# Retention's query and key projections as wide groups behind the visited ones, with the gate projections visited in their place

## The chip, the cores and the metric

The kernel runs on one core of one Trainium2 chip. The metric is the device time of one execution in microseconds, lower is better; the time before is the median of 3 runs. Times of single instructions, of waits and of stretches come from one execution taken by the hardware profiler.

The engines are called as the profile calls them: PE is the matrix engine (PEld its weight loads), DVE the vector engine, ACT the scalar engine, POOL the general-purpose engine, SP the queue that issues nearly all transfers. SBUF is the on-chip memory with 128 partitions; PSUM is the memory in eight banks into which PE writes, one bank holding 512 float32 columns.

## What is computed

One decoder layer with two token mixers and a gated convolutional feed-forward part, for 256 tokens of width 2048, in float32. The part that matters here is the projection `h @ w_in` and what takes its columns:

```python
h = modulate(rms_norm(x, g_norm1[l]), shift1, scale1)
p = h @ w_in[l]
rq, rk, rv, rg, hq, hf, hi, hg, ga, gb = jnp.split(p, split_at, axis=-1)

q_r = rope(rq.astype(f32).reshape(B, S, RET_H, RET_DK), positions)
k_r = rope(rk.astype(f32).reshape(B, S, RET_H, RET_DK), positions)
o_r = head_layer_norm(retention_chunkwise(q_r, k_r, v_r)).reshape(B, S, RET_H * RET_DV)
y_a = (o_r.astype(x.dtype) * jax.nn.silu(rg)) @ w_ret_o[l]
...
o_h = head_rms_norm(hgrn2_chunkwise(q_h, f_g, hi)).reshape(B, S, HG_H * HG_DV)
y_b = (o_h.astype(x.dtype) * jax.nn.silu(hg)) @ w_hg_o[l]

merged = jax.nn.sigmoid(ga) * y_a + jax.nn.sigmoid(gb) * y_b
x = x + gate1[:, None, :] * (merged @ w_out[l])
```

Each of rq, rk, rv, rg, hq, hf, hi, hg has 1024 columns, ga and gb 2048 each. `shift1` and `scale1` come from `silu(c) @ w_ada`, which is another 2048 x 12288 matrix. After this part come the second norm, the up projection with a causal convolution of three taps, and the down projection.

## The kernel before

**Number format.** Weights are read as float32. Each piece of weights is split into an upper part `wh` (ACT copies it to the format that PE multiplies fast, line 167) and a rest `wl` (DVE subtracts, line 172). Activations are split likewise, and lie side by side in one tile: `act[:, :T]` are the upper parts of all 256 tokens, `act[:, T:]` the rests. A product is upper times upper, rest of the activation times upper weight, and upper activation times rest of the weight; rest times rest is left out.

**Groups, pieces, buffers.** A group is 512 columns of a weight matrix, and has 16 k tiles of 128 rows. `pieces` (line 176) fetches two k tiles at a time: a DMA into one of 12 `raw` buffers, then `wh` and `wl` into one of 4 buffers each. A buffer is free again when the last matmul that reads it is done.

**Three forms of matmul.** `mm_rows` (190) keeps 128 tokens of an activation as the stationary operand and streams 512 columns of weights: for each k tile and each half of the tokens, upper and rest of the activation against `wh`, and the upper one against `wl`, so 6 matmuls of 512. The result has tokens in partitions. `mm_cols` (203) keeps 128 columns of weights and streams 256 tokens, 12 matmuls of 256 for each k tile; the result has columns in partitions, as rope and the scores want it. The up projection (`up_group`, 1071) has a third form: the weights are stationary, upper and rest of the activation are streamed together in one matmul of 512, and one matmul of 256 with `wl` follows; upper and rest land in two halves of a bank and are added when the bank is read.

**PSUM.** `pg` (89) gives a pair of banks, two pairs in all; `po` (95) gives one bank, four in all.

**The visited stage** (lines 837 to 869). `scale1` and `shift1` are made row by row on DVE from the transposed `w_ada`, two k tiles of the activation hT at a time, and projections start before hT is complete. The twelve groups of the tuple ATT are visited in turn; each visit multiplies the k tiles that are there and not yet done (1 to 5 of them), and `take` (790) adds the bank pair to the group's sum `accs[g]` in SBUF: ACT copies on the first visit, DVE adds on the later ones. When hT is complete, the groups are finished in the order of their number. The four groups in ROWS use `mm_rows`, the other eight `mm_cols`. As soon as the three groups of an HGRN2 half, or of a retention half, are finished, its generator is put into a background queue.

**Background.** `pump` is called after each pair of k tiles and takes steps of the generators in the queues by an estimate of their time, so that their instructions lie between those of the projections. Queue 0 is first in, first out: trigonometry, `hgrn` for two halves, `retention` for two halves, then the gating. Queue 1 has the products with `w_ada`. An instruction of the background stands in its engine's order like any other.

**Behind the visits** (874 to 898). The groups of `wb` (the gate projections hg and rg) run one after the other in `mm_rows` form, 16 k tiles each into one bank pair, and ACT writes Silu of the pair into a tile `gt` (883). Eight groups of `wab` for the branch gates follow in the same manner with Sigmoid (897). `hgrn` waits with its last part until its gate is there (670); `gating` multiplies retention's output by its gates.

**Tiles.** Sums, gates, rope's scratch, HGRN2's scratch and the like are blocks of 4 KiB per partition, of which there are 27 (`blk`, 73). A block is given back when the program drops its last name for it.

Of the kernel before, what the change touches and what calls it, by code (L numbers as in the profile page):

```python
# [16 lines left out]
AF = mybir.ActivationFunctionType  # L17
ALU = mybir.AluOpType

P = 128  # L20
D = 2048
T = 256
NT = T // P
KT = D // P
# [5 lines left out]
G = 512  # L30
# [8 lines left out]

C_RQ, C_RK, C_RV, C_RG, C_HQ, C_HF, C_HI, C_HG = (i * W1 for i in range(8))  # L40
C_GA, C_GB = 8 * W1, 8 * W1 + D
ATT = (C_HF, C_HF + G, C_HQ, C_HQ + G, C_HI, C_HI + G, C_RQ, C_RQ + G, C_RK, C_RK + G, C_RV, C_RV + G)
ROWS = (C_HI, C_HI + G, C_RV, C_RV + G)
GW = 2 * G
LEVELS = (64, 32, 16, 8, 4, 2, 1)
TWO_PI = 2.0 * math.pi
# [9 lines left out]
class Kernel:  # L56
# [146 lines left out]
    def mm_cols(self, ps, items, first, last):  # L203

        nc = self.nc
        cs = [slice(j * P, (j + 1) * P) for j in range(4)]
        outs = [ps[j // 2][:, j % 2 * T : (j % 2 + 1) * T] for j in range(4)]
        for i, (act, wh, _) in enumerate(items):
            for j in range(4):

                opens = first and i == 0 and j % 2 == 0
                nc.tensor.matmul(outs[j], lhsT=wh[:, cs[j]], rhs=act[:, :T], start=opens, stop=False, skip_group_check=True)  # L212
                nc.tensor.matmul(outs[j], lhsT=wh[:, cs[j]], rhs=act[:, T:], start=False, stop=False, skip_group_check=True)  # L213
        for i, (act, _, wl) in enumerate(items):
            for j in range(4):
                nc.tensor.matmul(outs[j], lhsT=wl[:, cs[j]], rhs=act[:, :T], start=False, stop=last and i == len(items) - 1, skip_group_check=True)  # L216

    def products(self, mm, ps, src, act, k0, kts, hold=0, first=True, last=True, gain=None):

# [306 lines left out]
    def hgrn(self, hb, hf, hq, v, gates):  # L526

        nc = self.nc

        f = self.blk([P, 4, T], name="f")  # L530
        k = self.blk([P, 4, T], name="k")
        b = self.blk([P, 4, T], name="b")
        nc.scalar.activation(f, hf, AF.Sigmoid)
        yield 3.0
        for h in range(4):
            g = slice(4 * hb + h, 4 * hb + h + 1)
# [16 lines left out]
        f = None  # L553
        q = self.blk([P, 4, T], name="q")
        nc.scalar.activation(q, hq, AF.Silu)
        yield 2.0
        at = self.blk([P, 4, T], name="at")
        nc.gpsimd.memset(at, 0.0)
# [9 lines left out]
        ps = self.po()  # L568
# [5 lines left out]
        ps = self.po()  # L574
# [4 lines left out]
        for c in range(2):  # L579
            dst = at[:, :, c * P : (c + 1) * P].rearrange("p h (z x) -> p h z x", x=32)  # L580
            msk = self.ident.bitcast(I32).rearrange("p (z x) -> p z x", x=32)[:, None].to_broadcast([P, 4, 4, 32])
            src = ps[:, 4 * c * 32 : 4 * (c + 1) * 32].rearrange("p (h x) -> p h x", h=4)[:, :, None, :].to_broadcast([P, 4, 4, 32])
# [3 lines left out]
        kt = self.blk([P, 4, T], name="kt")  # L586
        nc.gpsimd.memset(kt, 0.0)
        for lev, n in enumerate(LEVELS[:-2]):
# [15 lines left out]
            ps = self.po()  # L604
            for h in range(4):
                for c in range(2):
                    j = 2 * h + c
# [11 lines left out]
            if n >= 32:  # L619
                for z in range(0, P, 2 * n):  # L620
                    for c in range(2):
                        dst = at[z : z + n, :, c * P + z + n : c * P + z + 2 * n]
                        src = ps[z + c * n : z + (c + 1) * n, : 4 * n]
# [28 lines left out]
        ps = self.po()  # L652
        for z in range(2):
            for j in range(4 * z, 4 * z + 4):
                h, c = j // 2, j % 2
                for x in range(0, P, 32):
# [3 lines left out]
                        lhsT=kt[:, h, c * P + x : c * P + x + 32],  # L660
                        rhs=eq[:, j, :].rearrange("p (l x) -> p l x", l=2)[:, :, x // 2 : x // 2 + 16],
                        start=True,
                        stop=True,
# [3 lines left out]
            self.masked(at, len(LEVELS) - 2 + i, n, ps[:, : 8 * 32].rearrange("p (j l x) -> p j l x", j=8, l=2)[:, :, i, :])  # L667
            yield 0.9
        yield 2.8
        while len(gates) <= hb:  # L670
            yield None
        o = self.blk([P, NT, G], name="oh")
        for t in range(NT):
            ps = self.po()
# [85 lines left out]
    def run(self):  # L760
        nc, a = self.nc, self.a
# [23 lines left out]

        accs = [self.blk([P, NT, G] if c0 in ROWS else [P, 4, T], name="p") for c0 in ATT]
        done = [0] * len(ATT)
        mms = [self.mm_rows if c0 in ROWS else self.mm_cols for c0 in ATT]

# [14 lines left out]
        ps = [self.po2(), self.po2(), self.pg(), self.pg()][:FIRST]  # L804
        for k in range(2):
# [12 lines left out]
            for g in range(FIRST):  # L818
                if g >= ahead:
                    rests.append(self.rest(uppers[g] if g < len(uppers) else self.upper(a["wa"][g][:, k : k + 1, :], 1, G)))  # L820
                wh, wl = rests[g]
# [14 lines left out]

        work = 2 * FIRST
        g = FIRST
        att, gates = [], []
        small = False  # L840
        while min(done) < KT:
            if work > SMALL and not small:
                small = True
                self.small_loads(nc.sync, ("freq", "lbT", "lmask"))
                self.start(self.trig())
                self.start(self.lower_bound())
            have = min(KT, 2 + int((work - LAG) / ADA_EVERY))
            m = have - done[g]
            if m > 0:
                self.finish(*ada[:have])  # L850
                if g < RESIDENT:
                    self.products(mms[g], ps[g], a["wa"][g], act, done[g], m, first=False, last=have == KT)
                    if have == KT:
                        take(g, ps[g], True)
                else:
                    take(g, self.products(mms[g], self.pg(), a["wa"][g], act, done[g], m), done[g] == 0)
                done[g] = have
                work += m
                for hb in range(2):
                    for kind, first in ((self.hgrn, 0), (self.retention, 6)):  # L860
                        gs = [first + hb, first + 2 + hb, first + 4 + hb]
                        if g in gs and min(done[i] for i in gs) == KT:
                            self.pace(0, 14.0, 24)
                            att.append(self.start(kind(hb, *(accs[i] for i in gs), gates)))
            else:
                work += 0.5
            g = (g + 1) % len(ATT)
            if have == KT and done[0] < KT:
                g = min(i for i in range(len(ATT)) if done[i] < KT)
        self.xT = None  # L870
        del accs
        self.small_loads(nc.sync, ("gn2", "convw"))

# [2 lines left out]
        self.pace(0, 143.0, 88)  # L876
        self.pace(1, 68.0, 96)
        sgb, sga = [], []
        for j in range(4):
            ps = self.rows(a["wb"][j], act)  # L880
            gt = self.blk([P, NT, G], name="gt")
            for at, z in ps:
                nc.scalar.activation(gt[:, at, :], z, AF.Silu)
            gates.append(gt)

        og = [[], []]

# [6 lines left out]
        for j in range(8):  # L894
            gt = self.blk([P, NT, G], name="gt")
# [40 lines left out]
        for j in range(4):  # L936
            last = j == 3
            x1.append(self.load_rows(j))
            if not last:
                g = self.row(self.gate["gate1"], j, "g1")  # L940
            if j == 2:
                g3 = self.row(self.gate["gate1"], 3, "g1")
            elif last:
                g = g3
            ps = self.products(self.mm_rows, self.po2() if last else self.pg(), a["wout"][j], actm, 0, KT, hold=4 * last, gain=g if last else None)
            if last:
                g = None
# [49 lines left out]
        steps = []  # L997
# [173 lines left out]
def _pack(w):  # L1171

    k, n = w.shape
    return np.ascontiguousarray(w.reshape(k // P, P, n).transpose(1, 0, 2))


def _groups(w, starts):
    return np.stack([_pack(w[:, s : s + G]) for s in starts])
# [23 lines left out]
def _arrays(x, c, positions, w_ada, b_ada, g_norm1, w_in, w_ret_o, w_hg_o, w_out, hg_lb, g_norm2, w_up, conv_w, conv_b, w_down, g_final):  # L1202
    cols = lambda v: np.ascontiguousarray(v.reshape(-1, P).T)
    wada, win, wup = w_ada[0], w_in[0], w_up[0]
    out = {
        "xT": _pack(np.ascontiguousarray(x[0].T)),
        "c": c.reshape(1, D),
        "pos": positions.reshape(1, T),
        "gn1": cols(g_norm1[0]),
        "gn2": cols(g_norm2[0]),  # L1210
        "lbT": np.ascontiguousarray(hg_lb.reshape(2, HH, P).transpose(2, 0, 1)),
        "convw": np.ascontiguousarray(np.concatenate([conv_w[0], conv_b], axis=0).reshape(4, 2 * FT, P).transpose(2, 0, 1)),
        "gf": g_final.reshape(1, D),
        "xR": np.ascontiguousarray(x[0].reshape(NT, P, D).transpose(1, 0, 2)),
        "wb": _groups(win, [C_HG, C_HG + G, C_RG, C_RG + G]),
        "wab": _groups(win, [z + j * G for z in (C_GB, C_GA) for j in range(4)]),
        "whg": _groups(w_hg_o[0], [j * G for j in range(4)]),
        "wret": _groups(w_ret_o[0], [j * G for j in range(4)]),
        "wout": _groups(w_out[0], [j * G for j in range(4)]),
        "wdown": _groups(w_down[0], [j * G for j in range(4)]),  # L1220
        "wup": np.stack([_pack(np.concatenate([wup[:, 2 * i * P : 2 * (i + 1) * P], wup[:, FF + 2 * i * P : FF + 2 * (i + 1) * P]], axis=1)) for i in range(FT // 2)]),
    }
    out["wa"] = _groups(win, ATT)
    adaT = np.concatenate([wada.T, b_ada[0][:, None]], axis=1).reshape(6, KT, P, D + 1)
    out["ada1"] = np.ascontiguousarray(adaT[[1, 0]].transpose(1, 0, 2, 3))
    out["ada2"] = np.ascontiguousarray(adaT[[4, 3]].transpose(1, 0, 2, 3))
    out["gate1"] = adaT[2]
    out["gate2"] = adaT[5]
    out.update(_tables())
    return out  # L1230
# [22 lines left out]
```

## Time and profile before

| what | value |
|---|---|
| median of 3 runs | 1513.63 us (1513.56 to 1513.67) |
| profiled execution | 1513.78 us |
| its span, first to last instruction | 1512.0 us |
| mean granted PE clock | 0.998 |
| instructions | 23190 |
| busy: PE, DVE, ACT | 1496.0, 1206.4, 846.6 us |
| read from memory | 382.11 MB, 254 GB/s over the span |

How to read the rows that follow. A row of the waits names the engine and line that waited, then what it waited for, the total in us, the number of times and the longest. A row of the timeline has the start in us from the span's beginning, the duration, the engine, the line, the operation, what it writes and reads, and in brackets how long the engine was idle before it and what ended that. A row of the groups has line, engine, operation, tiles, shapes and count, then busy time in us and the mean duration in ns, then the idle time of the engine before these instructions. A row of the stretches has, for each engine, the busy time in us and in brackets the number of instructions that ran in it, then the granted clock, the DMAs' share and GB/s. Matmuls are pipelined: a recorded matmul of 256 columns lasts longer than the distance to the next one's start, so the cost of a matmul in a run of them is that distance.

### The profile page before, as it was taken

The numbers are of one execution on the slowest core, as the hardware profiler recorded it, in microseconds if no ns is written. First come the engines' busy times: TensorE is split into PE (matmuls) and PEld (weight loads), VectorE is DVE, ScalarE is ACT, GpSimd is POOL, SyncE is SP. The second block draws the span as 40 slices with busy tenths as digits, with TensorE's granted clock in tenths as the row PEclk, the third lists the DMA queues.
The fourth block names the chain that finished last, engine by engine and source line by source line (L and its number), as shares of the span: only waits on it lengthen the run. The fifth ranks groups of instructions, "written<-read, shape, count | busy, mean of one in ns | idle before, by whom it ended". The sixth has DMA issues, their size and how long they took to land.

```text
span 1512.0 us, 23190 instructions
## 1 busy us (share of the span) xinstructions
PE 1496.0 (99%) x8722; PEld 1288.2 (85%) x8722; DVE 1206.4 (80%) x1639; ACT 846.6 (56%) x1207; POOL 4.0 (0%) x8
## 2 busy tenths in 40 slices
PE   8999999999999999999999999999999999999997
PEld 6999999888888888888888888888888888888886
DVE  7899996997999877898977778778777769455794
ACT  6655454777875644455466555555655558344342
POOL 0000000000000000000000000000000000000000
PEclk9999999999999999999999999999999999999999
DMA  9999997777888889989847777777777766667651
GB/s 374 390 332 340 315 326 230 258 265 251 286 269 289 281 299 326 320 286 362 305 126 244 233 232 230 231 229 236 227 244 230 218 192 204 194 206 214 185 168 56
DMA packets 110996, 385.75 MB, mean 255 GB/s; under 512 B 12802, under 2 KB 13346, under 8 KB 110884
## 3 DMA queue, kind: packets, MB, share of 16 engines
q1 hardware_dynamic: 110016, 383.14, 76.8%
q8 instruction: 68, 1.11, 0.3%
q10 hardware_dynamic: 868, 1.13, 0.2%
q14 instruction: 44, 0.36, 0.1%
HBM read 382.11 MB, written 2.11 MB: 254 GB/s over the span
## 4 chain that ended last, share of the span: by engine, by line
PE 95%; DVE 3%; DMA 1%; ACT 1%; issue 0%; SPq 0%; DVEq 0%; ACTq 0%
PE pg L196 13%; PE pg L197 13%; PE pg L201 13%; PE po L1086 11%; PE pg L1086 10%; PE po L1088 5%; PE pg L1088 5%; PE po L201 3%; PE po L197 3%; PE po L196 3%; PE pg L212 3%; PE pg L213 3%; PE pg L216 3%; PE po L212 1%; PE po L213 1%; PE po L216 1%
## 5 line engine op out<-in xcount | busy, mean ns | idle before, releaser
L167 ACT ACTIVATE wh<-raw 128x1024 fp32r<-128x1024 f32 (+1 forms) x536 | 550.1, 1033 | 514.8 <-PE pg L197 181.1
L172 DVE TENSOR_TENSOR wl<-raw,wh 128x1024 fp32r<-128x1024 f32 (+1 forms) x536 | 634.0, 1189 | 236.0 <-ACT wh L167 232.7
L426 DVE SCALAR_TENSOR_TENSOR raw<-raw,sc 128x1024 f32<-128x1024 f32 x192 | 233.6, 1219 | 0.0
L1086 PE MATMUL po<-h2T,wh 128*128 128x512 f32 x704 | 221.1, 395 | 0.0
L1086 PE MATMUL pg<-h2T,wh 128*128 128x512 f32 x688 | 216.4, 396 | 0.0
L196 PE MATMUL pg<-wh,hT 128*128 128x512 f32 x512 | 202.8, 396 | 0.2 <-ACT p L794 0.2
L197 PE MATMUL pg<-wh,hT 128*128 128x512 f32 x512 | 200.0, 391 | 0.0
L1088 PEld LDWEIGHTS po<-h2T,wl 128*128 128x128 f32 x704 | 132.3, 188 | 31.2
L1088 PEld LDWEIGHTS pg<-h2T,wl 128*128 128x128 f32 x688 | 129.1, 188 | 31.1 <-DVE wl L172 0.5
L1088 PE MATMUL po<-h2T,wl 128*128 128x256 f32 x704 | 138.3, 278 | 0.0
L201 PE MATMUL pg<-wl,hT 128*128 128x512 f32 x512 | 137.4, 390 | 0.0
L1088 PE MATMUL pg<-h2T,wl 128*128 128x256 f32 x688 | 135.3, 278 | 0.1
L201 PEld LDWEIGHTS pg<-wl,hT 128*128 128x128 f32 x512 | 96.0, 188 | 20.4 <-DVE wl L172 0.2
L196 PEld LDWEIGHTS pg<-wh,hT 128*128 128x128 f32 x512 | 96.2, 188 | 19.9 <-ACT p L794 0.4
L197 PEld LDWEIGHTS pg<-wh,hT 128*128 128x128 f32 x512 | 96.2, 188 | 19.1
L1086 PEld LDWEIGHTS po<-h2T,wh 128*128 128x128 f32 x704 | 107.2, 189 | 0.0
L1086 PEld LDWEIGHTS pg<-h2T,wh 128*128 128x128 f32 x688 | 104.7, 189 | 0.0
L212 PE MATMUL pg<-hT,wh 128*128 128x256 f32 x384 | 95.2, 284 | 0.6 <-DVE p L796 0.6
L213 PE MATMUL pg<-hT,wh 128*128 128x256 f32 x384 | 95.1, 284 | 0.0
L212 PEld LDWEIGHTS pg<-hT,wh 128*128 128x128 f32 x384 | 74.1, 193 | 1.1 <-issue 0.8
L213 PEld LDWEIGHTS pg<-hT,wh 128*128 128x128 f32 x384 | 74.0, 193 | 0.3
L197 PE MATMUL pg<-wh,gs 128*128 128x512 f32 x176 | 68.6, 390 | 0.0
(250 smaller groups left out, 2062.7 us busy)
## 6 DMA issues: line engine op xcount, KB each, us to landing
raw<-in_wup SPq DMA_DIRECT2D x176, 512.0 KB, 4.4
raw<-in_wdown SPq DMA_DIRECT2D x88, 512.0 KB, 4.3
raw<-in_wa SPq DMA_DIRECT2D x80, 512.0 KB, 5.7
raw<-in_ada SPq DMA_DIRECT2D x64, 512.5 KB, 5.8
raw<-in_ada SPq DMA_DIRECT2D x64, 512.0 KB, 5.6
raw<-in_wab SPq DMA_DIRECT2D x64, 512.0 KB, 4.9
raw<-in_gate SPq DMA_DIRECT2D x32, 512.5 KB, 4.2
raw<-in_wb SPq DMA_DIRECT2D x32, 512.0 KB, 4.7
```

The lines of the kernel that those rows point to most:

```text
L167: self.pin(self.nc.scalar.activation(wh, raw, AF.Copy))
L172: self.last = self.nc.vector.tensor_tensor(wl, raw, wh.bitcast(F32), ALU.subtract)
L196: nc.tensor.matmul(ps[t], lhsT=act[:, hi], rhs=wh, start=first and i == 0, stop=False)
L197: nc.tensor.matmul(ps[t], lhsT=act[:, lo], rhs=wh, start=False, stop=False)
L201: nc.tensor.matmul(ps[t], lhsT=act[:, hi], rhs=wl, start=False, stop=last and i == len(items) - 1)
L212: nc.tensor.matmul(outs[j], lhsT=wh[:, cs[j]], rhs=act[:, :T], start=opens, stop=False, skip_group_check=True)
L213: nc.tensor.matmul(outs[j], lhsT=wh[:, cs[j]], rhs=act[:, T:], start=False, stop=False, skip_group_check=True)
L216: nc.tensor.matmul(outs[j], lhsT=wl[:, cs[j]], rhs=act[:, :T], start=False, stop=last and i == len(items) - 1, skip_group_check=True)
L426: dot = self.pin(nc.vector.scalar_tensor_tensor(raw[:, 0, :], raw[:, 0, :], 1.0, self.sc[:, u * GW : u * GW + w], ALU.mult, ALU.mult, accu ...
L1086: self.pin(nc.tensor.matmul(ps[j + z], lhsT=wh[:, cs[z]], rhs=act, start=kt == 0, stop=False, skip_group_check=bool(begun)))
L1088: nc.tensor.matmul(ps[j + z][:, :T], lhsT=wl[:, cs[z]], rhs=act[:, :T], start=False, stop=kt == KT - 1, skip_group_check=bool(begun))
```

## The change

ATT loses the four query and key groups of retention (`C_RQ`, `C_RK`) and gets the four gate groups in their places; the gates are visited in rows form, and when one is complete, ACT applies Silu to its sum in place. `gates` becomes a dictionary by number, and `hgrn` waits for its number in it. The names of `hf` and `hq` are dropped as soon as HGRN2 has read them.

Behind the visits, `wide_group` makes the four query and key groups, one after the other, in the wide form: both bank pairs belong to one group, four k tiles are taken at a time, and for each pair of banks the eight matmuls of 512 with `wh` come first and the eight of 256 with `wl` after them. Then each pair is evicted by an ACT copy of the half with the rests and a DVE addition of the upper half. After the second group the first half of retention is started, after the fourth the second. The host packs the four groups as `wk` in place of `wb`.

```diff
-ATT = (C_HF, C_HF + G, C_HQ, C_HQ + G, C_HI, C_HI + G, C_RQ, C_RQ + G, C_RK, C_RK + G, C_RV, C_RV + G)
-ROWS = (C_HI, C_HI + G, C_RV, C_RV + G)
+GATES = (C_HG, C_HG + G, C_RG, C_RG + G)
+ATT = (C_HF, C_HF + G, C_HQ, C_HQ + G, C_HI, C_HI + G, *GATES, C_RV, C_RV + G)
+ROWS = (C_HI, C_HI + G, *GATES, C_RV, C_RV + G)
+KEYS = (C_RQ, C_RK, C_RQ + G, C_RK + G)
...
+    def mm_wide(self, ps, items, first, last, pair):
+        nc = self.nc
+        for i, (act, wh, _) in enumerate(items):
+            for z in (pair, pair + 1):
+                nc.tensor.matmul(ps[z], lhsT=wh[:, z * P : (z + 1) * P], rhs=act, start=first and i == 0, stop=False)
+        for i, (act, _, wl) in enumerate(items):
+            for z in (pair, pair + 1):
+                nc.tensor.matmul(ps[z][:, :T], lhsT=wl[:, z * P : (z + 1) * P], rhs=act[:, :T], start=False, stop=last and i == len(items) - 1)
+
+    def wide_group(self, src, act):
+        nc = self.nc
+        pgs = [self.pg(), self.pg()]
+        ps = pgs[0][:2] + pgs[1][:2]
+        steps = list(range(0, KT, 4))
+        pieces = self.pieces(src, KT)
+        for k in steps:
+            items = [(act(kt), wh, wl) for _ in range(2) for kt, wh, wl in next(pieces)]
+            for pair in (0, 2):
+                self.mm_wide(ps, items, k == 0, k == steps[-1], pair)
+                self.pump()
+        out = self.blk([P, 4, T], name="p")
+        for pair in (0, 2):
+            dst = out[:, pair : pair + 2, :]
+            z = pgs[pair // 2][2]
+            nc.scalar.activation(dst, z[:, :, T:], AF.Copy)
+            nc.vector.tensor_tensor(dst, dst, z[:, :, :T], ALU.add)
+        return out
...
         nc.scalar.activation(f, hf, AF.Sigmoid)
+        hf = None
...
         nc.scalar.activation(q, hq, AF.Silu)
+        hq = None
...
-        while len(gates) <= hb:
+        while hb not in gates:
             yield None
...
+                if have == KT and ATT[g] in GATES:
+                    nc.scalar.activation(accs[g], accs[g], AF.Silu)
+                    gates[GATES.index(ATT[g])] = accs[g]
                 for hb in range(2):
-                    for kind, first in ((self.hgrn, 0), (self.retention, 6)):
-                        gs = [first + hb, first + 2 + hb, first + 4 + hb]
-                        if g in gs and min(done[i] for i in gs) == KT:
-                            self.pace(0, 14.0, 24)
-                            att.append(self.start(kind(hb, *(accs[i] for i in gs), gates)))
+                    gs = [hb, 2 + hb, 4 + hb]
+                    if g in gs and min(done[i] for i in gs) == KT:
+                        self.pace(0, 14.0, 24)
+                        begin(self.hgrn, hb, *(accs[i] for i in gs))
+                        for i in gs:
+                            accs[i] = None
...
-        for j in range(4):
-            ps = self.rows(a["wb"][j], act)
-            gt = self.blk([P, NT, G], name="gt")
-            for at, z in ps:
-                nc.scalar.activation(gt[:, at, :], z, AF.Silu)
-            gates.append(gt)
+        for hb in range(2):
+            begin(self.retention, hb, *[self.wide_group(a["wk"][2 * hb + i], act) for i in range(2)], v.pop(0))
```

More of the change, by code (lines that the diff above doesn't have):

```diff
@@ L838, in run, with begin @@
         g = FIRST
-        att, gates = [], []
+        att, gates = [], {}
+        def begin(kind, hb, *ins):
+            att.append(self.start(kind(hb, *ins, gates)))
         small = False
@@ L870, in run @@
         self.xT = None
+        v = accs[10:]
         del accs
@@ L1214, in _arrays @@
         "xR": np.ascontiguousarray(x[0].reshape(NT, P, D).transpose(1, 0, 2)),
-        "wb": _groups(win, [C_HG, C_HG + G, C_RG, C_RG + G]),
+        "wk": _groups(win, KEYS),
         "wab": _groups(win, [z + j * G for z in (C_GB, C_GA) for j in range(4)]),
```

## The prediction

> **What bounds the kernel now.** I read the page first: the span, the busy time of each engine and the chain that ended last.
>
> ```profile
> span 1512.0 us, 23190 instructions
> ...
> PE 1496.0 (99%) x8722; PEld 1288.2 (85%) x8722; DVE 1206.4 (80%) x1639; ACT 846.6 (56%) x1207; POOL 4.0 (0%) x8
> ...
> PE 95%; DVE 3%; DMA 1%; ACT 1%; issue 0%; SPq 0%; DVEq 0%; ACTq 0%
> ```
>
> PE is busy for 99% of the span and is 95% of the chain. A busy PE can still be waiting inside its pipeline, so the next view is that of the waits, for PE alone over the whole run (total, times, longest).
>
> ```profile
> engine line waited for: us in total, times, longest us
> PE po L264 <- DMA crow<-in_c: 2.3, 1, 2.3
> PE po L212 <- ACT hT L350: 1.9, 2, 1.2
> PE po L317 <- DVE rq L313: 1.6, 1, 1.6
> PE pg L1065 <- DVE h2T L398: 0.7, 1, 0.7
> PE po L618 <- DVE kt L602: 0.6, 1, 0.6
> PE pg L212 <- DVE p L796: 0.6, 1, 0.6
> PE pg L196 <- ACT p L794: 0.2, 1, 0.2
> PE po L213 <- DVE hT L355: 0.2, 1, 0.2
> ```
>
> These add up to 8.1 us, 5.8 of them in the three rows at the top, which belong to the start. So there is almost no idle time to win: the time is the number of matmuls times the distance between their starts. A change gains if it issues fewer or cheaper matmuls, and loses if DVE, ACT or the DMAs can no longer keep the next operands ready. How near those are to that point is read by stage. The visited stage runs to about 295 us, the four gate groups from there to about 390.
>
> ```profile
> core 0: us, PE busy (x) PEld busy (x) DVE busy (x) ACT busy (x) POOL busy (x), PEclk, DMA share, GB/s
> 20.00:100.00 80.00, 78.92 (x542) 73.68 (x542) 69.16 (x97) 49.79 (x75) 0.00 (x0) 1.00 1.00 371
> 100.00:180.00 80.00, 80.00 (x577) 75.96 (x576) 77.24 (x107) 43.33 (x63) 1.91 (x2) 1.00 0.97 339
> 180.00:260.00 80.00, 80.00 (x588) 76.47 (x588) 66.12 (x80) 37.33 (x54) 0.00 (x0) 1.00 0.85 281
> 260.00:293.00 33.00, 32.39 (x203) 29.14 (x202) 26.79 (x31) 26.21 (x30) 0.00 (x0) 1.00 0.71 231
> 293.00:335.00 42.00, 42.00 (x353) 34.24 (x352) 41.15 (x55) 29.35 (x42) 0.00 (x0) 1.00 0.83 276
> 335.00:377.00 42.00, 42.00 (x379) 34.65 (x378) 34.35 (x50) 33.21 (x54) 1.92 (x2) 1.00 0.76 255
> ```
>
> The granted clock is 1.00 in every stretch. DVE is 97% busy (77.24 of 80) from 100 to 180 us and 98% (41.15 of 42) from 293 to 335: those are the two narrow places. The DMAs moved 371 GB/s in the first stretch and 339 in the second, so there the bytes aren't at their limit.
>
> **The matmuls.** What one k tile (128 rows of weights, 512 columns) costs PE in each of the three forms is read from the timeline of PE, as the distance from one pair of k tiles to the next.
>
> ```profile
> 227.61 0.28 PE L212 MATMUL pg<-hT,wh 128*128 128x256 f32 x1
> ...
> 230.49 0.28 PE L212 MATMUL pg<-hT,wh 128*128 128x256 f32 x1
> ```
>
> Columns form (mm_cols, queries and keys now): 24 matmuls of 256 between these starts, 2.88 us, so 1.440 us per k tile and 0.120 each.
>
> ```profile
> 302.04 0.39 PE L196 MATMUL pg<-wh,hT 128*128 128x512 f32 x1
> ...
> 304.75 0.39 PE L196 MATMUL pg<-wh,hT 128*128 128x512 f32 x1
> ```
>
> Rows form (mm_rows, the gates before and after): 12 matmuls of 512, 2.71 us, so 1.355 per k tile and 0.226 each.
>
> ```profile
> 839.66 0.62 PE L1086 MATMUL pg<-h2T,wh 128*128 128x512 f32 x2
> 840.13 0.40 PE L1088 MATMUL pg<-h2T,wl 128*128 128x256 f32 x2
> ...
> 842.45 0.62 PE L1086 MATMUL po<-h2T,wh 128*128 128x512 f32 x2
> ```
>
> The up projection has the wide form that the change gives to queries and keys: 8 matmuls of 512 and 8 of 256 in 2.79 us, so 1.395 per k tile. All three forms stream 3072 columns per k tile; what differs is the number of matmuls, 12, 6 and 8. Two rows give both prices: if 0.120 is 256c+o and 0.226 is 512c+o, c is 0.414 ns and o 14 ns. Every matmul saved is worth about 14 ns, not its load of weights, which hides.
>
> The change turns 4 groups of 16 k tiles, 64 in all, from 12 matmuls into 4 of 512 and 4 of 256. In runs of eight like ones, as the new order issues them, the two single prices give 4x0.226+4x0.120=1.384; the up rows, the same mix in shorter runs, say 1.395. The saving is 64x(1.440-1.384)=3.6 us or 64x(1.440-1.395)=2.9. I take the middle, **3.2 us**. The gates cost 1.355 in either place. By stage: the visited one loses 64x(1.440-1.355)=5.4 us of PE, and what follows gains 64x(1.39-1.355)=2.2.
>
> The Trainium skill, page "TensorE: Matmul & The Clock Gate", section "Back-to-back issue gap", gives an isolated gap of N/2.4 ns plus 2.5 at full clock. By that an estimate for the k tile is 1.310 us in columns form and 1.300 in the wide form, and the saving would be 0.6 us in place of 3.2. The rows here have 14 ns where the page has 2.5, so the sum goes by the rows.
>
> **What else moves.** The visited stage still makes the same 53 visits with the same k tiles in each (counted by stepping through the loop of lines 841 to 869), one eviction per visit, and the same background work tied to k tiles and not to time. Its transfers are as many and as large; the SP queue only has the gate groups' loads where the query and key groups' were. A round of the twelve groups at one k tile takes 8x1.440+4x1.355=16.94 us now and 16.60 after, 2.0% less, in which DVE, ACT and DMA must do as much. DVE at 97% would be at 98.5%: it fits, barely. I cost this at 0 to 0.5 us and take 0.
>
> The evictions and gates need these rows, the last two from the groups of ACT between 293 and 500 us.
>
> ```profile
> L172 DVE TENSOR_TENSOR wl<-raw,wh 128x1024 fp32r<-128x1024 f32 x504 | 613.6, 1221 | 232.8 <-ACT wh L167 231.9
> ...
> L796 DVE TENSOR_TENSOR p<-p,pg 128x1024 f32<-128x1024 f32 x37 | 45.0, 1217 | 14.5 <-PE pg L216 11.7 <-PE pg L201 2.5
> ...
> L1035 DVE TENSOR_TENSOR gp<-pg,g 128x512 f32<-128x512 f32 x10 | 6.4, 684 | 1.6 <-PE pg L201 1.6
> ```
>
> ```profile
> 314.01 0.60 ACT L572 ACTIVATE a<-po 128x512 f32<-128x512 f32 x1 [0.69 <-PE po L570]
> ```
>
> ```profile
> L883 ACT ACT_TABLE_LOAD x4 | 5.1, 1283 | 0.1
> ...
> L883 ACT ACTIVATE gt<-pg 128x1024 f32<-128x1024 f32 x4 | 4.1, 1028 | 0.0
> ```
>
> The four Silus of the gates (1.03 us, each with a table load of 1.28 and mostly another one back) leave the stage behind the visits and come into the end of the visits, as four of 1.03 from SBUF. At that end PE has one visible wait now:
>
> ```profile
> 280.11 0.35 PE L212 MATMUL pg<-hT,wh 128*128 128x256 f32 x1 [0.61 <-DVE p L796]
> ```
>
> By the same count three gate groups get visits of a single k tile there. Such a visit costs DVE an addition of 1.22 and a half-size split, more than PE's 1.36. Since PE's part shrinks by 0.085, about 3x0.085=**0.25 us** more shows as waiting. The Silus queue ahead of the copies (wh) for the last two visits; 26.21 of 33 us are busy on ACT there, and 3x1.03 plus one load of 1.28, 4.4 us, go into 6.8. I take nothing for that; its bounds are 0 and 1.5.
>
> In the wide groups each group is evicted by two copies on ACT (0.60) and two additions on DVE (0.68 from PSUM). For four groups that is 4.8 us more on ACT, less than the Silus and loads that left, and 5.5 more on DVE, where nothing left. DVE is idle for 8.5 us of 293 to 377, so it fits, but in the second half only. Bank pair 0 is evicted while PE runs the last 16 matmuls of pair 2, 8x0.226+8x0.120=2.77 us; the eviction takes 0.60+0.68=1.28. I cost it at 0; bounds 0 and 3.3 per group, below.
>
> The weights' lead is what I'd not call free. Four buffers hold wh and wl, two k tiles each. In rows form a buffer goes back after 2.7 us; a wide step keeps two until its end at 5.6 us, so the reserve falls from as much as 10.8 us to between 5.6 and 11.2, by where in the step it is needed. One place uses most of it:
>
> ```profile
> 362.09 1.04 ACT L167 ACTIVATE wh<-raw 128x1024 fp32r<-128x1024 f32 x1
> ...
> 372.51 1.05 ACT L167 ACTIVATE wh<-raw 128x1024 fp32r<-128x1024 f32 x1
> ```
>
> For 9.4 us (363.13 to 372.51) ACT makes no copy, since one HGRN2 block ends and the next begins. PE doesn't wait there now. The background is paced by k tiles, so after the change this falls into the fourth wide group. A gate's Silu and load (2.31 us) are gone from it, and 7.1 us are left against 5.6 to 11.2: a stall of 0 to 1.5. I take **0.75**. Rope and retention stand behind both HGRN2 blocks in the background queue, as now, and the last query and key group is done before their turn, so nothing waits for them.
>
> **The sum.** -3.2+0.25+0.75=-2.2 us. The profiled execution took 1513.78 us, its span 1512.0, and 1.8 lie around it. 1513.78-2.2=1511.6; the profiled one lies 0.15 above the median of the three runs, 1513.63, so the forecast for the median is **1511.4 us**.
>
> **The rivals.**
> All covers hold: nothing new is waited for, the saving is the larger one (3.6), and the 0.6 wait at the end of the visits goes with the shifted order. That gives -3.2 to -4.2, 1509.4 to 1510.4. For it: PE waited for nothing between 42 and 277 us, and ACT is relieved. Against it: 97% and 98% of DVE.
>
> Late bank pairs, the slower one: at the four ends of wide groups the eviction stands behind other work on ACT and DVE, and PE can't open pair 0 of the next group, nor anything queued behind it. Worst case from the rows: a table load 1.28, a copy of 1.05, the eviction's 0.60, two splits of 1.22, the addition of 0.68 make 6.05 us, 3.3 above the cover of 2.77; four times 13. At half of that, 6.6 us, the time is 1513.6-3.2+6.6=1517.0. It decides from 1.6 us a group, an eviction of 4.3 us. For it: DVE is full from 293 to 335. Against it: in the group row of L796, DVE sat idle before these additions for 14.5 us in all, mostly until PE was done, so evictions are not queued late now.
>
> The visits don't get faster because DVE is the bound there: the 5.4 us of PE turn into waiting for wl, and the 2.2 of the wide form stay, so 1513.6+2.2=1515.8 at most. Against it: 97 is not 100, and from 180 to 260 us DVE had 14 us free.
>
> Loads of weights in the open, by the group of the loads for wl in rows form:
>
> ```profile
> L201 PEld LDWEIGHTS pg<-wl,hT 128*128 128x128 f32 x512 | 96.0, 188 | 20.4 <-DVE wl L172 0.2
> ```
>
> Were a load of 0.188 not hidden behind the matmul before it, four loads less per k tile would give 64x4x0.188=48 us, so 1465. The starts 0.120 apart exclude it: less than one load. The same page of the Trainium skill, section "The mechanism", says that a load overlaps matmuls in flight only where the row group differs; the trace speaks against it here, where every load fills the whole array.
>
> **How the numbers follow.** About 0.2%, 3 us, is what a measurement of this kernel can tell from no change. The forecast's case, -3 to 0 us, has 0.48; all covers hold 0.33; late bank pairs 0.12; visits bound by DVE 0.06; open loads 0.01. Faster takes the second and the last, 0.34; slower the late pairs, 0.12; the same the rest, 0.54. The range reaches from the covers that hold, 1509.4, to DVE as the bound, 1515.8, and leaves out 0.13.
>
> **What would show it.** Right: starts of the wide matmuls 0.23 and 0.12 apart, visits of gates with 0.226, the visited stage some 5 us shorter, the four groups behind it some 2 us longer, waits of PE still below 10 us. Wrong: PE waiting for wl in 80 to 180 us (DVE the bound), or for DVE or ACT on pg at the first matmul of a wide group (late pairs), or a wide k tile well off 1.39 us.

## The result, and the profile after

| | before | after |
|---|---|---|
| median | 1513.85 us (21 runs) | 1511.24 us (21 runs) |
| lowest to highest | 1513.42 to 1514.91 | 1510.81 to 1512.56 |
| profiled span | 1512.0 us | 1509.5 us |

The ratio is 0.9984, with a 95% interval of 0.9978 to 0.9990. That is 2.6 us less, 0.16%, just inside the 0.2% which the prediction set as the bound of no change; the forecast was 1511.4.

The page after, from its first part and the chain that ended last:

```profile
span 1509.5 us, 22703 instructions
...
PE 1493.7 (99%) x8466; PEld 1275.5 (84%) x8466; DVE 1211.9 (80%) x1647; ACT 841.7 (56%) x1210; POOL 4.0 (0%) x8
...
PE 93%; DVE 3%; ACT 1%; issue 1%; DMA 1%; SPq 0%; DVEq 0%; ACTq 0%
```

PE has 256 matmuls less (8722 to 8466, 4 for each of 64 k tiles), DVE 8 instructions and 5.5 us more (the additions that evict), ACT 4.9 us less. The new lines of the program are 225 (the wide matmul of 512), 228 (that of 256 with wl), 246 and 247 (the eviction's copy and addition); 198, 199 and 203 are the rows form, 830 is the addition of a visit.

The waits of PE over the whole run, after:

```profile
PE po L296 <- DMA crow<-in_c: 2.5, 1, 2.5
PE po L214 <- ACT hT L382: 1.7, 2, 1.2
PE po L349 <- DVE rq L345: 1.6, 1, 1.6
PE pg L1104 <- DVE h2T L430: 0.7, 1, 0.7
PE pg L198 <- DVE p L830: 0.6, 1, 0.6
PE pg L225 <- DVE p L247: 0.2, 1, 0.2
PE pg L198 <- ACT p L828: 0.2, 1, 0.2
PE po L215 <- DVE hT L387: 0.2, 1, 0.2
```

The list has the same length and nearly the same sum as before, 7.7 us against 8.1. One entry is new, the 0.2 us for a bank pair of the wide groups (L247). One is gone: the 0.6 us in which a matmul of HGRN2 (line 618 before) waited for DVE.

Where the time went is read from three points that both kernels have: the first matmul behind the visits, the first and the last Sigmoid that empties a group of wab, and the end. The first rows are from the timeline of PE, before and after; the second pair is that of the line with the Sigmoid, its durations and the first and last start.

```profile
293.88 0.39 PE L196 MATMUL pg<-wh,hT 128*128 128x512 f32 x1
```

```profile
289.50 1.30 PE L225 MATMUL pg<-hT,wh 128*128 128x512 f32 x5
```

```profile
L897 ACT ACTIVATE gt<-pg x8: 1004/1029/1033, 417.4 to 589.8; 128x1024 f32<-128x1024 f32 x8
```

```profile
L936 ACT ACTIVATE gt<-pg x8: 1007/1027/1033, 415.5 to 587.3; 128x1024 f32<-128x1024 f32 x8
```

| stretch | before | after | difference |
|---|---|---|---|
| start to the end of the visits | 293.9 | 289.5 | -4.4 |
| the four groups behind them, and the first group of wab | 123.5 | 126.0 | +2.5 |
| the other seven groups of wab | 172.4 | 171.8 | -0.6 |
| from there to the end of the span | 922.2 | 922.2 | 0.0 |

So the visits gained less than the forecast's 5.15 us, the wide groups cost less than its 2.95, and 0.6 us came from a place that it hadn't named.

What a wide k tile costs is read from the timeline of PE after, in a stretch without other work:

```profile
300.65 2.00 PE L225 MATMUL pg<-hT,wh 128*128 128x512 f32 x8
302.49 1.11 PE L228 MATMUL pg<-hT,wl 128*128 128x256 f32 x8
303.44 2.00 PE L225 MATMUL pg<-hT,wh 128*128 128x512 f32 x8
```

From one run of eight to the next are 2.79 us, 1.84 for eight of 512 and 0.95 for eight of 256. A step of four k tiles is two of these, one for each bank pair, so a k tile costs 2x2.79/4=1.395 us: exactly the up projection's price, and not the 1.384 that single prices would give. Eight like matmuls in a row are not cheaper than two.

### The profile page after: what moved, and what is told of

It is laid out like the page before. It is cut to its first block, busy times and chain, and to the rows that moved or that the text cites. A ratio compares the mean times of both kernels' runs of the same rounds, so it can differ in the third digit from the quotient of the medians.

```text
span 1509.5 us, 22703 instructions
## 1 busy us (share of the span) xinstructions
PE 1493.7 (99%) x8466; PEld 1275.5 (84%) x8466; DVE 1211.9 (80%) x1647; ACT 841.7 (56%) x1210; POOL 4.0 (0%) x8
## 4 chain that ended last, share of the span: by engine, by line
PE 93%; DVE 3%; ACT 1%; issue 1%; DMA 1%; SPq 0%; DVEq 0%; ACTq 0%
PE pg L198 13%; PE pg L203 13%; PE pg L199 13%; PE po L1125 11%; PE pg L1125 10%; PE po L1127 5%; PE pg L1127 5%; PE pg L225 4%; PE po L198 3%; PE po L203 3%; PE po L199 3%; PE pg L228 2%; DVE wl L174 1%; DVE raw L458 1%; PE po L218 1%
## 5 line engine op out<-in xcount | busy, mean ns | idle before, releaser
L199 PE MATMUL pg<-wh,gs 128*128 128x512 f32 x176 | 68.6, 390 | 0.0
L198 PE MATMUL pg<-wh,gs 128*128 128x512 f32 x176 | 68.5, 389 | 0.0
L198 PE MATMUL po<-wh,gs 128*128 128x512 f32 x176 | 68.5, 389 | 0.0
L199 PE MATMUL po<-wh,gs 128*128 128x512 f32 x176 | 68.5, 389 | 0.0
L225 PE MATMUL pg<-hT,wh 128*128 128x512 f32 x256 | 65.1, 396 | 0.2 <-DVE p L247 0.2
```

The lines of the kernel that those rows point to most:

```text
L198: nc.tensor.matmul(ps[t], lhsT=act[:, hi], rhs=wh, start=first and i == 0, stop=False)
L199: nc.tensor.matmul(ps[t], lhsT=act[:, lo], rhs=wh, start=False, stop=False)
L225: nc.tensor.matmul(ps[z], lhsT=wh[:, z * P : (z + 1) * P], rhs=act, start=first and i == 0, stop=False)
```

## The experiments

The theory, A: PE is the bound, a matmul costs 0.414 ns per column and 14 ns of its own, and so the form decides; where the groups stand in the order is worth little. The rivals: B, the gain is the order, or ACT's relief; and for the four k tiles of a step, whether they matter as cover for the eviction (F), in every step (G), or do harm by a shorter lead of the weights (C). All kernels were timed beside the kernel before, whose median was then 1513.96 or 1513.97.

**The form undone, the order kept.** The four groups behind the visits are made in columns form.

```diff
-        pgs = [self.pg(), self.pg()]
-        ps = pgs[0][:2] + pgs[1][:2]
...
+        ps = self.products(self.mm_cols, self.pg(), src, act, 0, KT)
         out = self.blk([P, 4, T], name="p")
...
+        for at, z in self.parts(ps, False):
+            nc.scalar.activation(out[:, at, :], z, AF.Copy)
```

> The order of the change is kept (gates visited, queries and keys behind the visits), only their form is undone: mm_cols, 12 matmuls of 256 per k tile, one bank pair and one copy per group. Theory A (the gain is 14 ns for each matmul saved, the order is worth nothing): 64x(1.440-1.395)=2.9 us slower than the changed kernel, less the 0.4 us that PE waited there for a bank pair, so 2.5 slower and level with the kernel before, 1513.7. Theory B (the gain is the order and the relief of ACT, which loses the gates' Silu and table loads behind the visits): as fast as the changed kernel, 1511.2.

Measured: 1513.13 us, ratio to before 0.9994 (0.9985 to 1.0002). That is 1.9 us slower than the changed kernel (all its 11 times lie above all 21 of the changed kernel), and 0.8 faster than the kernel before, which its interval doesn't tell from nothing. Its first matmul behind the visits and its first Sigmoid of wab:

```profile
289.44 0.28 PE L214 MATMUL pg<-hT,wh 128*128 128x256 f32 x1
```

```profile
L925 ACT ACTIVATE gt<-pg x8: 1008/1029/1032, 417.6 to 589.3; 128x1024 f32<-128x1024 f32 x8
```

The visits end where they end after the change, the stretch behind them takes 128.2 us against 126.0, and the seven groups 171.7. So the form is worth 2.2 us in its stretch, as A says, and B has at most the 0.6 to 0.7 of the seven groups.

**The number of matmuls alone.** Each wide matmul of 512 is cut into two of 256 with the same weights, so there are 256 matmuls more, each with a load of weights of its own. The columns, the order, the banks and the evictions stay the same.

```diff
-                nc.tensor.matmul(ps[z], lhsT=wh[:, z * P : (z + 1) * P], rhs=act, start=first and i == 0, stop=False)
+                for u in range(2):
+                    half = slice(u * T, (u + 1) * T)
+                    nc.tensor.matmul(ps[z][:, half], lhsT=wh[:, z * P : (z + 1) * P], rhs=act[:, half], start=first and i == u == 0, stop=False, skip_group_check=True)
...
```

> The changed kernel with each matmul of 512 in the wide groups cut into two of 256 with the same weights: 12 matmuls per k tile in place of 8, the same columns streamed, the same order, banks, evictions, ACT and DVE work. Theory A (a matmul costs its columns at 0.414 ns and 14 ns): 1.440 per k tile, 64x0.045=2.9 us slower than the changed kernel, 1514.1, all of it between 290 and 390 us. If the gain of the form lay elsewhere (order, evictions, one copy of ACT less): 1511.2.

Measured: 1513.80 us, ratio 0.9997 (0.9988 to 1.0006), 2.6 slower than the changed kernel.

```profile
290.33 1.35 PE L227 MATMUL pg<-hT,wh 128*128 128x256 f32 x10
```

```profile
L938 ACT ACTIVATE gt<-pg x8: 1008/1026/1029, 418.8 to 590.4; 128x1024 f32<-128x1024 f32 x8
```

The stretch of the wide groups takes 128.4 us against 126.0, 2.4 more (the first Sigmoid starts at 418.75 us here, at 415.53 in the changed kernel). Its matmuls are slower, so the cover is longer, and the wait of 0.4 us for a bank pair, shown below, shrinks to 0.2. That makes the price of 256 matmuls with their loads 2.6 us, 10 ns each; the prices of 1.440 and 1.395 per k tile give 11 ns. So A's 14 ns are too many in this form, but this is the term that carries the change, and it was changed by itself here. That the visits end 0.8 us later than in the changed kernel has another reason: in this profile the granted clock was at 0.50 for 3.4 us from 27.5 us on, ahead of the first visit in rows form.

**Two k tiles per bank pair in place of four.**

```diff
-        steps = list(range(0, KT, 4))
+        steps = list(range(0, KT, 2))
...
-            items = [(act(kt), wh, wl) for _ in range(2) for kt, wh, wl in next(pieces)]
+            items = [(act(kt), wh, wl) for kt, wh, wl in next(pieces)]
...
-                self.pump()
+                self.pump(0.5)
```

> Wide form with two k tiles per bank pair in place of four. Matmuls and their prices are the same; pair 2 covers the eviction of pair 0 for 4x0.227+4x0.12=1.39 us in place of 2.77, and buffers of weights go back after 2.8 us in place of 5.6. Theory A (evictions take 0.60+0.68=1.28 us behind PE unless ACT is in another piece of work): within 0.5 us of the changed kernel, 1511.2 to 1511.7. Theory C (the lead of the weights, which four k tiles shorten, costs 0.75 us): 0.4 to 0.75 faster, 1510.5.

Measured: 1514.26 us, ratio 1.0002 (0.9993 to 1.0010): 3.0 slower than the changed kernel, the whole gain. Neither expectation holds. The waits of PE between 280 and 400 us:

```profile
PE pg L225 <- DVE p L247: 1.3, 3, 0.7
PE pg L198 <- DVE p L247: 0.9, 1, 0.9
```

PE waits at the groups' ends for the addition that evicts a bank pair, 2.2 us in all: 1.39 us of cover are not enough for two instructions of 1.28. From the end of the last matmul on pair 0 to the end of the addition that empties it, 2.3, 2.5, 2.1 and 2.3 us pass at the four ends, 3.5 us more than the cover in all. PE fills a part of that with matmuls of the background; the stretch is 3.3 us longer than in the changed kernel.

**One k tile per bank pair**, the up projection's order, with 0.70 us of cover.

```diff
-        steps = list(range(0, KT, 4))
+        steps = list(range(0, KT, 2))
...
-            items = [(act(kt), wh, wl) for _ in range(2) for kt, wh, wl in next(pieces)]
-            for pair in (0, 2):
-                self.mm_wide(ps, items, k == 0, k == steps[-1], pair)
-                self.pump()
+            for kt, wh, wl in next(pieces):
+                for pair in (0, 2):
+                    self.mm_wide(ps, [(act(kt), wh, wl)], kt == 0, kt == KT - 1, pair)
+            self.pump()
```

> Wide form k tile by k tile, two of 512 and two of 256 for each pair, the up projection's order. The cover of pair 0's eviction is then 2x0.227+2x0.12=0.70 us. Theory A: the k tile costs 1.395 as before and each of the four boundaries 0.7 to 0.9 us, so 2.8 to 3.6 slower than the changed kernel, 1514 to 1514.8. If runs of eight like matmuls are what makes the wide form cheap (1.384 against 1.395): another 0.7 us slower.

Measured: 1517.43 us, ratio 1.0023 (1.0013 to 1.0032): 6.2 slower than the changed kernel, more than expected. Its waits, in the same stretch:

```profile
PE pg L225 <- DVE p L247: 3.3, 2, 2.7
PE pg L198 <- DVE p L247: 1.2, 1, 1.2
```

One boundary alone costs 2.7 us. The 4.5 of these rows don't make up the 6.2. Most of the rest stands right behind that wait, which ends at 369.33 us. These are rows of PE, and the stretch from 370.2 to 373.5 us:

```profile
370.16 1.05 PE L225 MATMUL pg<-hT,wh 128*128 128x512 f32 x2
371.01 0.63 PE L228 MATMUL pg<-hT,wl 128*128 128x256 f32 x2
371.44 1.05 PE L225 MATMUL pg<-hT,wh 128*128 128x512 f32 x2
```

```profile
370.20:373.50 3.30, 3.30 (x11) 2.80 (x11) 3.19 (x4) 2.51 (x3) 0.00 (x0) 0.50 0.43 104
```

The granted clock is 0.50 there. Two matmuls of 512 take 0.85 us (370.16 to 371.01) in place of 0.46, two of 256 take 0.43 in place of 0.24. From 370.16 to 373.55 us PE does what takes 1.86 us at the usual distances, so this costs 1.5 us. That the wait brought the clock down is likely, but no run varied it by itself.

**The order of the pairs turned round in the last step, meant to take the cover away.** In the last step of a group pair 2 comes first.

```diff
-            for pair in (0, 2):
+            for pair in (0, 2) if k < steps[-1] else (2, 0):
```

> In the last step of each wide group pair 2 comes first and pair 0 last, so that the next group, which opens with pair 0, has nothing to cover its eviction. Theory A: each of the four boundaries costs the eviction, 1.28 us and some hand-over, 1.4 to 1.6 us, so 5.6 to 6.4 us in all: 1516.8 to 1517.6. Theory D (the evictions are queued behind other work, as the late bank pairs of the prediction): 2.5 to 4 us for each, 1521 and more. If the cover is worth nothing: 1511.2.

Measured: 1510.78 us, ratio 0.9981 (0.9972 to 0.9989), not to be told from the changed kernel, and the one wait for L247 is 0.2 us as there. No expectation for a lost cover holds. The cover was not lost, as these rows of the first boundary show, the copies that evict (ACT) and the first matmuls of the second group (PE):

```profile
308.82 0.60 ACT L246 ACTIVATE p<-pg 128x512 f32<-128x512 f32 x1 [2.60 <-PE pg L228]
...
313.49 0.58 ACT L246 ACTIVATE p<-pg 128x512 f32<-128x512 f32 x1
```

```profile
313.19 2.00 PE L225 MATMUL pg<-hT,wh 128*128 128x512 f32 x8
```

The second group opens at 313.19 us, before the second copy has started, so it opens on the bank pair that was evicted first. It is the same at the other two boundaries between wide groups (339.43 and 365.88 us, with the second copy ending at 339.90 and 366.27). The swap only mirrors the two pairs. This run says nothing on the price of an eviction; the two before and the two that follow do.

**Four k tiles at the end of a group only**, steps of two elsewhere; and the reverse, **two at the end only**.

```diff
-        steps = list(range(0, KT, 4))
+        steps = [(0, 2), (2, 2), (4, 2), (6, 2), (8, 2), (10, 2), (12, 4)]
...
```

```diff
-        steps = list(range(0, KT, 4))
+        steps = [(0, 4), (4, 4), (8, 4), (12, 2), (14, 2)]
...
```

> Wide groups in steps of two k tiles, only the last step of each group has four, so that pair 0's eviction has 2.77 us of cover again. The run with two throughout was 3.0 us slower than the changed kernel, and PE waited 2.2 us for the additions that evict. Theory F (the four k tiles matter only at the end of a group, as cover for the eviction): level with the changed kernel, 1511.0 to 1511.8. Theory G (they matter in every step, by longer runs of like matmuls or by how ACT and DVE prepare the weights): slower by most of the 3.0, 1513.5 to 1514.

> The reverse: steps of four k tiles, the last four k tiles in two steps of two, so 1.39 us of cover at the end of each group. Theory F: as slow as two throughout, 1513.4 to 1514.2. Theory G: nearly as fast as the changed kernel, 1511.2 to 1512.

Measured: 1512.08 us for four at the end (ratio 0.9987, 0.9978 to 0.9996) and 1514.63 for two at the end (1.0005, 0.9996 to 1.0014). The last step's length decides most of it: 2.6 us lie between the two, against 3.0 between four and two throughout. F holds in kind and G doesn't, though both kernels came out 0.3 to 0.4 us above F's ranges. The first is 0.8 slower than the changed one, which their intervals don't separate; its profile has one wait of 0.7 for L247. The waits of the second between 60 and 400 us:

```profile
PE pg L225 <- DVE p L247: 1.9, 2, 1.5
PE pg L198 <- ACT wh L169: 0.6, 1, 0.6
PE pg L198 <- DVE p L247: 0.6, 1, 0.6
```

2.5 us of them are for an eviction. (The middle row is the end of the visits.)

**More work for DVE in the visits.** One more multiplication of 0.68 us for each of 13 k tiles of hT; its result is not used.

```diff
             self.modulated(act(k), self.xT[k // 4][:, k % 4, :], k, s1, t1)
+            if k > 2:
+                x = self.xT[k // 4][:, k % 2 * 2 : k % 2 * 2 + 2, :]
+                nc.vector.tensor_tensor(self.s2([P, 2, T], name="spare"), x, x, ALU.mult)
```

> The changed kernel with one more DVE multiplication of 128x512 (0.68 us, its result unused) for each k tile of hT from the fourth on, 13 in the visited stage, 8.9 us of DVE in all. There DVE was busy for 78.1 of 80 us between 100 and 180 us in the changed kernel and for 67.5 of the next 80. Theory H (DVE is nearly the bound of the visits, and what is put on it beyond the free 2 us appears on PE as waiting): some 6 of the 13 fall between 90 and 180 us, 4.1 us, so 2 to 3 us slower than the changed kernel, 1513.2 to 1514.3, in waits between 100 and 180 us. If PE's lead covers it: within 0.4 us, 1511.2 to 1511.6.

Measured: 1511.93 us, ratio 0.9986 (0.9978 to 0.9995), 0.7 slower than the changed kernel, which their intervals don't separate: a miss for H by its size, and a little more than PE's lead would leave. Two of its stretches, with the columns of the prediction's view, and the one wait for weights in the visits (from the view between 60 and 400 us):

```profile
100.00:140.00 40.00, 39.03 (x249) 35.32 (x248) 39.75 (x57) 18.37 (x28) 0.95 (x1) 1.00 0.95 330
140.00:180.00 40.00, 40.00 (x187) 33.47 (x186) 39.78 (x55) 22.69 (x34) 0.05 (x1) 1.00 0.95 328
```

```profile
PE pg L203 <- DVE wl L174: 1.0, 1, 1.0
```

DVE is busy for 99% of 80 us and PE waits once, for 1.0 us. Counted from the first matmul of the first visit in rows form, the visits take 0.9 us longer than in the changed kernel.

**Less work for DVE in the visits.** The subtraction that makes the rests of hT goes to POOL from the fourth k tile on.

```diff
-        self.pin(self.nc.vector.tensor_tensor(dst[:, T:], h, dst[:, :T].bitcast(F32), ALU.subtract))
+        low = self.nc.gpsimd if k > 2 else self.nc.vector
+        self.pin(low.tensor_tensor(dst[:, T:], h, dst[:, :T].bitcast(F32), ALU.subtract))
```

> The changed kernel with the subtraction that makes the rests of hT (128x256, 0.42 us on DVE) on POOL for the 13 k tiles from the fourth on: 5.5 us less on DVE in the visited stage. PE lost 0.4 us between 100 and 140 us in the changed kernel, where it lost nothing before the change. Theory H: those 0.4 us come back, 1510.8, if POOL makes no rest late; theory I (POOL takes several us for one, and hT's k tiles come later than their visits): slower by up to 1 us for each k tile that is late.

Measured: 1510.94 us, ratio 0.9980 (0.9971 to 0.9988), 0.3 faster than the changed kernel, which the intervals don't separate. The sign is H's. Counted as above, the visits are shorter by 0.15 us, so less than half of the 0.4 came back. POOL's line, from the trace:

```profile
L388 POOL TENSOR_TENSOR hT<-h,hT x13: 740/796/1638, 54.1 to 240.1; 128x256 fp32r<-128x256 f32 x13
```

None of these versions beats the changed kernel by more than its uncertainty.

## Why the prediction was right, and where its steps were off

**The matmuls: right.** The forecast priced the saving at 3.2 us, the middle of 2.9 (up projection's rows) and 3.6 (single prices in longer runs). The wide k tile measured 1.395, so the value was 2.9, and the order in runs of eight added nothing. The split of the wide matmuls shows the term by itself: 2.4 us in its stretch, 2.6 with what the longer cover gave back.

**The visits: right in kind, 0.65 too large, and DVE was not free.** Forecast was -5.4+0.25=-5.15 us. The table has -4.4, but it counts from the start of the span, where executions differ. The first visit in rows form starts here, before and after:

```profile
32.57 0.50 PE L196 MATMUL pg<-wh,hT 128*128 128x512 f32 x1 [0.22 <-ACT p L794]
```

```profile
32.71 0.50 PE L198 MATMUL pg<-wh,hT 128*128 128x512 f32 x1 [0.22 <-ACT p L828]
```

From there to the end of the visits are 261.3 and 256.8 us, so 4.5 less; in the seven experiments that leave the visits as they are it is 256.7 to 256.8. A part of the missing 0.65 is the rows form's price: with 1.36 (6x0.2267 by the starts in its runs) in place of 1.355 it is 64x0.08=5.1. The other 0.6 are distances between PE's starts above these prices, 1.2 us in all before and 1.8 after. The largest new one is a wait for DVE, the term costed at 0 of 0 to 0.5. These rows are PE's and DVE's:

```profile
118.73 0.28 PE L214 MATMUL po<-hT,wh 128*128 128x256 f32 x1
119.08 0.73 PE L203 MATMUL pg<-wl,hT 128*128 128x512 f32 x2
```

```profile
117.81 1.22 DVE L174 TENSOR_TENSOR wl<-raw,wh 128x1024 fp32r<-128x1024 f32 x1
```

The split is done at 119.03 and its first matmul starts at 119.08, 0.35 behind the start of the one before it in place of 0.12, and the next distance is 0.1 too long as well: 0.3 us. The rest are 0.1 us or less at a place. DVE was busy for 78.08 of 80 us between 100 and 180 us, 97.6%, where 77.24 had been.

```profile
100.00:180.00 80.00, 79.93 (x438) 69.62 (x437) 78.08 (x109) 42.53 (x63) 1.91 (x2) 1.00 0.96 337
```

How near DVE came is better read from the lead of its splits, from the end of a split to the first matmul that reads it. Over the 29 splits between 100 and 180 us it was at least 1.7 us before the change (median 3.4); over the 30 after it, the least is 0.06 and the median 1.6. So the sign that the prediction had named for DVE as the bound, PE waiting for wl between 80 and 180 us, did show, for 0.3 us. The rival itself, with 0.06, did not happen, and the run with more DVE work shows that there was still some room. The wait at the end of the visits, which the 0.25 was for, was 0.63 us in place of 0.61.

**The weights' lead: the step that failed.** It was costed at 0.75 us in the fourth wide group. The pause of ACT came back there, from 359.22 to 368.05 us, 8.8 us without a copy; the rows are ACT's.

```profile
358.17 1.05 ACT L169 ACTIVATE wh<-raw 128x1024 fp32r<-128x1024 f32 x1
...
362.68 1.28 ACT L565 ACT_TABLE_LOAD   x1
363.97 1.06 ACT L565 ACTIVATE f<-p 128x1024 f32<-128x1024 f32 x1
364.94 0.58 ACT L246 ACTIVATE p<-pg 128x512 f32<-128x512 f32 x1
...
368.05 2.00 ACT L169 ACTIVATE wh<-raw 128x1024 fp32r<-128x1024 f32 x2
```

PE didn't wait for weights, though. What was late was the bank pair, the step costed at 0. These rows are PE's and DVE's:

```profile
362.14 1.11 PE L228 MATMUL pg<-hT,wl 128*128 128x256 f32 x8
...
366.29 0.97 PE L225 MATMUL pg<-hT,wh 128*128 128x512 f32 x3 [0.25 <-DVE p L247]
```

```profile
365.55 0.69 DVE L247 TENSOR_TENSOR p<-p,pg 128x512 f32<-128x512 f32 x1 [0.26 <-ACT p L246]
```

Pair 0 is complete at 363.25. Its copy stands on ACT behind a table load and a Sigmoid of the next HGRN2 block and starts at 364.94; the addition ends at 366.24, 3.0 us after the pair was complete, and the cover was 2.77. The eight matmuls of 256 that start at 364.93 leave room for the next at 365.89 (8x0.12); it starts at 366.29, 0.4 us late, of which the view shows 0.25 as idle time.

**The late bank pairs: the right mechanism, held off by the four k tiles.** The prediction gave it 0.12 and put its point at 1.6 us per group. With 2.77 us of cover it shows once, for 0.4. With 1.39 it costs 2.2 us of waits and 3.0 us of time, with 0.70 it costs 6.2 and makes the kernel slower than before. The step behind it that failed is the price of an eviction, put at 0.60+0.68=1.28 us. From the end of the last matmul on pair 0 (309.19, 336.45, 363.25 and 386.12 us) to the end of its addition, 2.1, 2.4, 3.0 and 2.5 us passed at the four ends, so it was queued behind other work at each of them, and 2.77 us of cover hid that at three. The prediction had read from the 14.5 us of idle time before the additions of the visits that evictions are not queued late. That sum is of a few: by the view of that line, 13 of the 37 additions had waited for PE.

```profile
PE pg L216: 11.7, 8
PE pg L201: 2.5, 5
```

The other 24 had next to none.

**What the forecast did not name:** 0.6 us in the groups of wab, where the wait of HGRN2's matmul for DVE is gone from PE's list. It is there with the columns form too (171.7 us for the seven groups), so it doesn't belong to the wide form. Which moved instruction took it away was not tried.

So the total, -2.6 us against -2.2, came out closer than its terms, and that is luck: the visits gave 0.65 less than forecast and the start of the profiled execution 0.1 less, the wide groups cost 0.45 less, and 0.6 came unforeseen.

## What to carry to other kernels

Where PE's starts lie at a constant distance, price a change by the number of matmuls and their columns, from starts in runs without gaps, and check the mix itself where the trace has it: the up projection's rows gave the wide price to the last digit. When a form takes all banks of a buffer pair at once, the next group waits for the eviction, so let the last matmuls of the other pair be longer than the eviction and one piece of foreign work on each engine in it. A neighbour engine that is 97% busy is not yet a bound; ask how far its results lie ahead, and take that lead, not the busy share, as what is left.

## What the runs showed that was not expected

An eviction of two instructions, 0.58 and 0.69 us, took 3.0 us behind one table load and one Sigmoid; with 1.39 us of cover, more than the two instructions together, PE still lost 2.2 us at the groups' ends. Soon after a wait of 2.7 us the granted clock was 0.50 for 3.4 us, and PE's work in them took 1.5 us more than usual. A subtraction of 128x256 takes POOL 0.80 us (median of 13) where DVE takes 0.42, and could run beside the other engines without a visible cost.
